# Modulation steps of the first layer: from the input projections into the attention, five to a head, and four raw tiles in the out projection

## The chip, the cores and the metric

The kernel runs on one core of one Trainium2 chip. The metric is the device time of one execution in microseconds (us); runs are compared by their median. The five engines each work through their own list of instructions in order: TensorE (PE in the profile, with its weight loads as PEld), VectorE (DVE), ScalarE (ACT), GpSimd (POOL) and SyncE (SP), which only issues transfers.

## What is computed

One inference step of a two-layer diffusion trunk, for 512 sample tokens and 128 prompt tokens with a model width of 1024. Cut to what matters here:

```python
def adaln(cvec, w_mod, b_mod):                       # six vectors of 1024 for each of two conditionings
    m = jax.nn.silu(cvec) @ w_mod + b_mod
    return m.reshape(cvec.shape[0], N_MOD, D_MODEL)[:, :, None, :]

for l in range(DEPTH):                               # two layers, the first with MLA attention
    mp, ms = adaln(c_ctx[None, :], w_mod[l], b_mod[l]), adaln(c, w_mod[l], b_mod[l])
    hs = modulate(rmsnorm(xs, norm_mix[l]), ms[:, 0], ms[:, 1])
    os_ = even_latent(hs, ...)                       # input projections, 12 heads, out projection w_out
    xs = xs + ms[:, 2] * os_
    hs = modulate(rmsnorm(xs, norm_ffn[l]), ms[:, 3], ms[:, 4])
    xs = xs + ms[:, 5] * conv_ffn(hs, ...)
```

The same is done for the prompt tokens with `mp`. The outputs are both token sets after a last norm and the new cache entries.

## The kernel before, in words

Activations are kept transposed, as eight tiles of 128 channels by W = 642 columns (512 sample columns, two of padding, 128 prompt columns), and are worked on in two halves, of 352 and 290 columns. All products are float32 split into a high and a low part: each term is three matmuls (`mm3`), and every weight tile that arrives raw is split by a cast on ScalarE (`whi` or `wo`) and a subtraction on VectorE or POOL (`wlo`, or the second `wo`; line 113).

The first layer goes through these stages: `start` (first norm, with modulation vectors 0 and 1), `mla_in` (the input projections, the norms of the low-rank queries `q` and of the latent `c`), `mla` (attention), `out_proj` (output projection, residual, the sum for the next norm), `ffn`. The second layer follows.

**Modulation steps.** Each vector `m` of a layer is a matrix-vector product for two conditionings, taken in steps. A step (`mod_step`) takes one raw tile of `w_mod`, 128 rows k by n columns, scales it by the conditioning and adds it to two accumulators: for the first conditioning one product on VectorE (line 316), for the second a scaling on ScalarE (313) and an addition on POOL (314). In mode "d" both are on VectorE; the first step of a sum (k = 0) runs on ScalarE alone (310), or in mode "d" on VectorE. Eight steps make the sum for n columns; the eighth is followed by two transposes (325) and two sums (326) on VectorE, the end of a sum. `mod_finish` turns a finished vector into columns with four small matmuls in two passes each (337) and adds the bias (275); inside `mods` it does so once a vector has been ready for five steps. `mods_in` gives a stage its number of steps, its ring of raw tiles and the queue that loads them: a load is issued when a step has freed its tile.

Before, `mla_in` runs the 16 steps of vector 2 (two sums of 512 columns) with a ring of three on ScalarE's queue, at the places marked `m` and `m.d` in the list `MLA_IN`; the attention runs the 32 steps of vector 4 (four sums of 256 columns) with a ring of three on SP; the out projection and the feed-forward run the rest (vectors 3 and 5, then layer 1) in steps of 512 columns with a ring of two on SP.

**Order.** In `mla_in` and `mla` the order of each engine's work is written out by hand. `MLA_IN` is a list of steps such as `p.q0.1` (projection q0, second half), `zc` (copy out), `sq` (squares), `sm` (sum of squares), `ln`, `nw` (root and Newton step), `sc` (scale and cast to the high part), `lo` (low part), `xc` (copy of a pooling projection out of its accumulator), `f` and `r` (fetch and split a weight), `m`. `MLA_UNITS` holds two such lists for the two halves of a head; unit t = 2 x head + half computes scores and exponentials of its own, and transposes and weighs those of the unit before. Heads with new keys (`k`) are those of odd number up to 9; new queries (`q`) are made up to head 9. Steps `m` run from t = 2 on, while there are any.

The out projection and the feed-forward are ordered by the scheduler of the framework, from the order of the program and its estimates; SP is ordered by it everywhere. `out_proj` makes eight outputs j for the first half and eight for the second; in its first pass each j loads its x tile and its weight tile (raw tiles: three in all). After each output come two modulation steps. `normed` holds the norm of the first half: the end of the modulation vectors, the sum of squares (359), then scale and shift (424, 437, 438) on VectorE and ScalarE, whose results `ha` and `hb` are the operands of the feed-forward.

Of the kernel before, what the change touches and what calls it, by code (L numbers as in the profile page):

```python
# [8 lines left out]
F32 = mybir.dt.float32  # L9
# [9 lines left out]
KT = 8  # L19
# [27 lines left out]

MLA_IN = """
m p.kr.0 m.d p.c0.0 p.kr.1 r.q0 f.q2 m.d rt p.c0.1 zc.c0 m.d m.d cx p.c1.0 p.c1.1 p.q0.0 sq.c0 zc.c1 r.q1 m.d sq.c1 sm.c r.q2 m.d m.d
f.xp0 ln.c f.wk f.xp1 nw.c.0 m nw.c.1 p.q0.1 p.q1.0 zc.q0 sq.q0 sc.c.1.0 p.q1.1 sc.c.1.1 lo.c.1.1 sc.c.0.1 r.wk p.q2.0 sc.c.0.0 rc  # L50
lo.c.0.0 zc.q1 lo.c.0.1 sq.q1 lo.c.1.0 m.d r.xp0 kp.1 kp.0 ke.1 p.q2.1 f.wq m.d r.xp1 f.wv ke.0 xz m zc.q2 p.xp0.0 m sq.q2 m sm.q p.xp0.1
ln.q r.wv nw.q.0 xc.0 xa.0 sc.q.0.0 p.xp1.0 r.wq p.xp1.1 iv.0 sc.q.0.1 xb.0 lo.q.0.0 sc.q.0.2 lo.q.0.1 nw.q.1 lo.q.0.2 m.d xm.0 sc.q.1.0
sc.q.1.1 xc.1 lo.q.1.0 sc.q.1.2 lo.q.1.1 xa.1 lo.q.1.2 xb.1 iv.1 m.d xm.1
"""


# [6 lines left out]
MLA_UNITS = ["""  # L63
v0.1 m sc.0 wl.0 sc.1 we.2 ou tu.0 tu.1 wl.1 ex.0 ex.1 lo.0 q lo.1 pm.1 no.0 no.1 tu.2 we.0 k m m pm.0 pa lo.2 ke v0.0 v qs ve we.1
""", """
sc.0 sc.1 pm.0 tu.0 lo.0 v0.1 tu.1 we.2 ou ex.0 wl.0 no.0 ex.1 v0.0 q tu.2 lo.1 no.1 wl.1 lo.2 we.0 m k ke we.1 v pa ve pm.1 qs
"""]
MLA_MODS = 32

ODD_NA = ["""  # L70
s.1 je s.0 m.0 j.3 jr.d t.0 pt l.0 j.5 m.1 je.d s.2 w.0 t.1 sp e.0 pl l.1 t.2 s.3 w.1 m.2 e.1 l.2 pw j.4 po sv r.1 br t.3 m.3 w.2 e.2
# [18 lines left out]
class Trunk:  # L90
# [359 lines left out]
    def out_proj(self, pool, l, oT, xsrc, after, early=()):  # L450

        nc = self.nc
        x, w, h, normed = [], [], self.acts(), None
        with self.pool(f"wout{l}") as wpool:
            for half in range(2):
                acc = None
                for j in range(KT):
                    if not half:
                        xt = self.T(pool, "x", [P, W], F32, 8)
                        nc.sync.dma_start(xt, xsrc[:, j, :])  # L460
                        x.append(xt)
                        split = early[j] if j < len(early) else self.fetch(self.i["w_out"][l, j], D, *(() if j < 3 else (wpool, ("wo", "wo"), 10)))
                        w.append(split(nc.gpsimd if j in OUT_LO[l] else nc.vector))
                    ps = self.PS("mm")
                    self.proj_half(ps, w[j], oT, half, order=(6, 7, 0, 1, 2, 3, 4, 5) if l == 0 else range(KT))
                    self.add_x(l, 2, j, x[j], ps[:, C0:C1], *HALF[half])
                    xj = x[j][:, slice(*HALF[half])]
                    acc = self.add_sqs(pool, half, j, xj, acc, nc.gpsimd if j in OUT_SQ[l][half] else nc.vector)
                    after()
                    if j == 1 and normed:  # L470
                        normed()

                def normed(half=half, acc=acc):
                    self.mod_finish("b")
                    self.norm_half(pool, h, x, acc, half, l, 3, 4)

            normed()
        return x, h
# [313 lines left out]
    def mla(self, pool, oT, wq):  # L792
# [97 lines left out]
        u1 = u2 = None  # L890
        for t in range(2 * MH + 2):
            hd, hf = divmod(t, 2)
            if t == 2:
                self.mod_finish("tr")
            u = None
            if hd < MH:
                u = Unit()
# [558 lines left out]
    def run(self):  # L1456
        tc, nc, i, o = self.tc, self.nc, self.i, self.o
        with ExitStack() as st:
# [35 lines left out]
            self.sink = const("sink", [P, 8], nc.sync)  # L1494
            self.nsink = cp.tile([P, 8], F32, name="nsink")
            nc.vector.tensor_scalar(out=self.nsink, in0=self.sink, scalar1=-1.0, scalar2=None, op0=ALU.mult)
            self.todo = deque(self.mods_of(0, (2,), 512) + self.mods_of(0, (4,), 256) + self.mods_of(0, (3, 5), 512))
            oT = self.acts()
            with self.pool("mla") as pool:
                self.mp, self.Q, self.V, self.wq, self.pm, self.pw = pool, {}, {}, {}, [], []  # L1500
# [4 lines left out]
                with self.psums(mla), self.pool("mla_att") as self.ap:  # L1505
                    self.qtab = self.T(self.ap, "qtab", [P, W])
                    nc.sync.dma_start(self.qtab, i["qtab"])
                    self.T(self.ap, "q32", [P, HA], F32, 2)
                    self.T(self.ap, "q", [P, W], F32R, 6)
                    wq = self.fetch(i["w_qk"][0], D)  # L1510
                    self.mods_in(self.ap, MLA_MODS, 3, nc.sync)
                    bias_full = self.bias_table(cp, dpool)
                    with tc.manual_schedule(engines=ENGINES):
                        self.mla(self.ap, oT, wq)
                        self.mod_finish("tr")
                        w_out = [self.fetch(i["w_out"][0, j], D) for j in range(3)]
            with self.psums(wide), self.pool("ffn0") as pool:
                self.todo.extend(self.mods_of(1, range(6), 512))
                self.mods_in(pool, len(self.todo), 2, nc.sync)
                x, h = self.out_proj(pool, 0, oT, i["xT"], lambda: self.mods_until("b", MODS_OUT, (0, 5)), w_out)  # L1520
                nh = self.acts()

                def tail(half, acc):
                    if half:
                        for k in range(KT):
                            nc.sync.dma_start(xd[:, k, :], x[k])
                    self.mod_finish("b")
                    self.norm_half(pool, nh, x, acc, half, 1, 0, 1)

                self.ffn(pool, 0, h, x, lambda n: self.mods("b", n), tail)  # L1530
# [796 lines left out]
```

## Time and profile before

| | |
|---|---|
| median of 3 runs | 1700.57 us (1700.29 to 1706.34) |
| the profiled execution | 1703.3 us, span 1701.5 us, clock 0.972 |
| TensorE busy | 1584.5 us (93%) |
| VectorE busy | 1260.4 us (74%) |
| ScalarE busy | 929.0 us (55%) |
| POOL busy | 770.5 us (45%) |
| transfers | 175.62 MB, 103 GB/s |

How to read it: the span is the time from the first to the last instruction of the program in the profiled execution. Times in the trace count from the span's start. In rows of groups stand line, engine, operation, output <- inputs, count, then busy time, mean in ns, and the idle time of the engine before them with what ended it. In rows in order of time stand start, duration and, in brackets, the idle time before and its releaser. Rows of waits name who waited for whom: us in total, times, the longest. Windows give the busy time of each engine with the number of its instructions, then TensorE's granted clock, the share of the DMA engines and GB/s.

### The profile page before, as it was taken

Reading aid. Unit: us, or ns where it says so; the run is one execution under the profiler, and the core shown is the slowest. Engines: PE = TensorE matmul, PEld = TensorE weight load, DVE = VectorE, ACT = ScalarE, POOL = GpSimd, SP = SyncE. Lnnn points to the kernel's source line nnn. Section 1 sums busy time; section 2 is a strip of 40 time slices with the busy share of each in tenths; the row PEclk is TensorE's granted clock in tenths of the full one; section 3 lists DMA queues with packets and bytes.
Section 4 is the critical chain, followed back from the end, with each engine's and each line's share of the span. In section 5 each row is a group of like instructions: output and inputs, shape, how many; then the busy total and the mean of one; then the engine's idle time right before and its main releaser. Section 6 shows DMA issues by size and latency. Waiting matters only on the chain.

```text
span 1701.5 us, 28135 instructions
## 1 busy us (share of the span) xinstructions
PE 1584.5 (93%) x10349; PEld 1512.7 (89%) x10349; DVE 1260.4 (74%) x2190; ACT 929.0 (55%) x1792; POOL 770.5 (45%) x704
## 2 busy tenths in 40 slices
PE   8878888889999999999997999998997999999996
PEld 2777777788899999999997999987997999999996
DVE  4896788768999778977638777776687666776766
ACT  3554777655555345544345678886565344444445
POOL 2154777554234332534063234663325456555543
PEclk9997999998999999999999999998999999999999
DMA  9431212044344444544225211114222122222221
GB/s 342 137 100 56 63 50 80 14 160 140 112 143 151 159 137 139 159 142 137 84 86 183 70 42 58 53 43 163 75 82 85 63 89 88 78 78 74 78 73 63
DMA packets 79032, 175.62 MB, mean 103 GB/s; under 512 B 11598, under 2 KB 29342, under 8 KB 78894
## 3 DMA queue, kind: packets, MB, share of 16 engines
q1 hardware_dynamic: 76398, 169.55, 30.9%
q10 hardware_dynamic: 2304, 4.20, 0.8%
q8 instruction: 82, 1.34, 0.3%
q14 instruction: 56, 0.46, 0.1%
q0 software_dynamic: 192, 0.07, 0.0%
HBM read 166.71 MB, written 8.03 MB: 103 GB/s over the span
## 4 chain that ended last, share of the span: by engine, by line
PE 49%; DVE 16%; issue 6%; ACT 5%; DMA 5%; POOL 1%; SPq 0%; DVEq 0%; ACTq 0%; POOLq 0%
PE p L1594 24%; PE mm L137 19%; DMA mraw<-in_w_mod_dram 4%; DVE wlo L113 2%; DVE acc L316 2%; PE sc L1209 1%; PE tr L1247 1%; PE o L1259 1%; DVE u L511 1%; DVE nt L424 1%; ACT whi L117 1%; DVE ha L438 1%; DVE g L113 1%; DVE v L1997 1%; ACT mt L313 1%
## 5 line engine op out<-in xcount | busy, mean ns | idle before, releaser
L314 POOL TENSOR_TENSOR acc<-acc,mt 128x512 f32<-128x512 f32 x115 | 175.5, 1526 | 266.1 <-ACT mt L313 251.3
L137 PE MATMUL mm<-ha,whi 128*128 128x352 f32 (+1 forms) x1168 | 287.5, 328 | 4.7 <-ACT ha L437 4.6
L137 PE MATMUL mm<-hb,whi 128*128 128x290 f32 (+1 forms) x1168 | 244.2, 302 | 1.1 <-ACT hb L437 1.1
L137 PEld LDWEIGHTS mm<-ha,whi 128*128 128x128 f32 (+1 forms) x1168 | 202.4, 190 | 6.5 <-ACT ha L437 4.7
L316 DVE SCALAR_TENSOR_TENSOR acc<-mraw,cs,acc 128x512 f32<-128x512 f32 (+1 forms) x165 | 169.7, 1035 | 47.5 <-DMA mraw<-in_w_mod_dram 45.9
L137 PEld LDWEIGHTS mm<-hb,whi 128*128 128x128 f32 (+1 forms) x1168 | 192.8, 191 | 4.0 <-issue 2.7
L137 PE MATMUL mm<-ha,wlo 128*128 128x352 f32 (+1 forms) x584 | 188.9, 324 | 0.0
L113 POOL TENSOR_TENSOR wlo<-raw,whi 128x1024 fp32r<-128x1024 f32 (+3 forms) x46 | 98.3, 2142 | 175.1 <-ACT whi L117 116.3
L137 PE MATMUL mm<-hb,wlo 128*128 128x290 f32 (+1 forms) x584 | 174.7, 299 | 0.0
L113 POOL TENSOR_TENSOR w<-raw,w 128x512 fp32r<-128x512 f32 (+1 forms) x68 | 90.3, 1339 | 172.9 <-ACT w L117 164.8
L137 PE MATMUL mm<-g,whi 128*128 128x352 f32 (+1 forms) x704 | 157.8, 311 | 7.0 <-DVE x L447 5.2
L117 ACT CAST whi<-raw 128x1024 fp32r<-128x1024 f32 (+3 forms) x117 | 116.0, 996 | 68.5 <-PE mm L137 52.0
L313 ACT ACTIVATE mt<-mraw,cs 128x512 f32<-128x512 f32 x115 | 81.7, 720 | 113.4 <-DMA mraw<-in_w_mod_dram 101.0
L1594 PE MATMUL p<-g,d 128*128 128x320 f32 (+1 forms) x912 | 140.0, 312 | 0.9 <-POOL d L113 0.9
L1594 PEld LDWEIGHTS p<-g,d 128*128 128x128 f32 x912 | 136.4, 189 | 2.3 <-POOL d L113 2.1
L1594 PE MATMUL p<-hb,w 128*128 128x322 f32 (+1 forms) x816 | 129.0, 313 | 7.4 <-DVE cg L1966 6.7
L1594 PEld LDWEIGHTS p<-hb,w 128*128 128x128 f32 x816 | 123.4, 191 | 8.3 <-DVE cg L1966 6.9
L137 PEld LDWEIGHTS mm<-g,whi 128*128 128x128 f32 x704 | 118.4, 189 | 9.5 <-ACT ha L437 3.9
L1594 PE MATMUL p<-ha,w 128*128 128x322 f32 x768 | 122.7, 314 | 1.5 <-ACT ca L1960 1.5
L1594 PEld LDWEIGHTS p<-ha,w 128*128 128x128 f32 x768 | 117.5, 192 | 1.9 <-ACT ca L1960 1.8
L137 PEld LDWEIGHTS mm<-hb,wlo 128*128 128x128 f32 (+1 forms) x584 | 112.5, 193 | 0.0
L137 PEld LDWEIGHTS mm<-ha,wlo 128*128 128x128 f32 (+1 forms) x584 | 110.1, 188 | 0.5
(332 smaller groups left out, 3763.1 us busy)
## 6 DMA issues: line engine op xcount, KB each, us to landing
raw<-in_w_up_dram SPq DMA_DIRECT2D x90, 512.0 KB, 3.6
mraw<-in_w_mod_dram SPq DMA_DIRECT2D x128, 256.0 KB, 2.9
raw<-in_w_out_dram SPq DMA_DIRECT2D x19, 512.0 KB, 4.0
raw<-in_w_in_odd_dram SPq DMA_DIRECT2D x18, 512.0 KB, 3.6
mraw<-in_w_mod_dram SPq DMA_DIRECT2D x16, 512.0 KB, 8.8
raw<-in_w_down_dram SPq DMA_DIRECT2D x16, 512.0 KB, 3.6
draw<-in_w_down_dram SPq DMA_DIRECT2D x40, 192.0 KB, 2.4
raw<-in_w_down_dram SPq DMA_DIRECT2D x16, 384.0 KB, 3.1
```

The source lines that it names most:

```text
L113: (engine or self.nc.vector).tensor_sub(lo, src, Fv(hi))
L117: self.nc.scalar.copy(hi, src)
L137: self.pe = self.nc.tensor.matmul(out, lhsT=l, rhs=r, start=k == 0, stop=k == n - 1)
L313: nc.scalar.activation(t, raw, AF.Copy, scale=s)
L314: nc.gpsimd.tensor_add(acc, acc, t)
L316: nc.vector.scalar_tensor_tensor(out=acc, in0=raw, scalar=s, in1=acc, op0=ALU.mult, op1=ALU.add)
L424: self.nc.vector.scalar_tensor_tensor(out=t[:, c], in0=x[k][:, c0:c1][:, c], scalar=self.mod[l][:, ma, k, v : v + 1], in1=rs[:, c], op0=AL ...
L438: nc.vector.scalar_tensor_tensor(out=lo[:, c], in0=t[:, c], scalar=ss, in1=Fv(hi[:, c]), op0=ALU.add, op1=ALU.subtract)
L511: nc.vector.scalar_tensor_tensor(out=u[:, 1:W], in0=ps[:, 0 : W - 1], scalar=cw[:, j, 0:1], in1=u[:, 1:W], op0=ALU.mult, op1=ALU.add)
L1209: nc.tensor.matmul(ps[:, c : c + n], lhsT=u.Q[:, a], rhs=x[e], start=e == 0, stop=e == 1)
L1247: nc.tensor.transpose(tp[:, j * P : (j + 1) * P], u.p[b][:, x : x + P], self.ident)
L1594: self.t.pe = self.nc.tensor.matmul(ps[:, 0:n], lhsT=l_, rhs=r[:, 0:n], start=first and m == 0, stop=last and m == count - 1, skip_group_c ...
```

## The change

`MLA_IN` loses the last eight of its 16 modulation steps, `xc.1` and `lo.q.0.2` move ahead of `nw.q.1`, and the second list of `MLA_UNITS` gets a second `m`, so that a head has five. Vector 2 is now one sum of 512 columns (in `mla_in`) and two of 256 (in the attention, eight steps each); the attention has 48 steps, from t = 2 to t = 20. Two calls of `mod_finish` go. In the out projection two x tiles are loaded ahead, each further weight tile is fetched right after a split, the norm of the first half stands behind output 2 of the second half instead of output 1, and the ring of raw modulation tiles, there and in the feed-forward, is four.

```diff
 m p.kr.0 m.d p.c0.0 p.kr.1 r.q0 f.q2 m.d rt ...
-f.xp0 ln.c f.wk f.xp1 nw.c.0 m nw.c.1 p.q0.1 p.q1.0 zc.q0 sq.q0 sc.c.1.0 p.q1.1 sc.c.1.1 lo.c.1.1 sc.c.0.1 r.wk p.q2.0 sc.c.0.0 rc
-lo.c.0.0 zc.q1 lo.c.0.1 sq.q1 lo.c.1.0 m.d r.xp0 kp.1 kp.0 ke.1 p.q2.1 f.wq m.d r.xp1 f.wv ke.0 xz m zc.q2 p.xp0.0 m sq.q2 m sm.q p.xp0.1
-ln.q r.wv nw.q.0 xc.0 xa.0 sc.q.0.0 p.xp1.0 r.wq p.xp1.1 iv.0 sc.q.0.1 xb.0 lo.q.0.0 sc.q.0.2 lo.q.0.1 nw.q.1 lo.q.0.2 m.d xm.0 sc.q.1.0
-sc.q.1.1 xc.1 lo.q.1.0 sc.q.1.2 lo.q.1.1 xa.1 lo.q.1.2 xb.1 iv.1 m.d xm.1
+f.xp0 ln.c f.wk f.xp1 nw.c.0 nw.c.1 p.q0.1 p.q1.0 zc.q0 sq.q0 sc.c.1.0 p.q1.1 sc.c.1.1 lo.c.1.1 sc.c.0.1 r.wk p.q2.0 sc.c.0.0 rc
+lo.c.0.0 zc.q1 lo.c.0.1 sq.q1 lo.c.1.0 r.xp0 kp.1 kp.0 ke.1 p.q2.1 f.wq r.xp1 f.wv ke.0 xz zc.q2 p.xp0.0 sq.q2 sm.q p.xp0.1
+ln.q r.wv nw.q.0 xc.0 xa.0 sc.q.0.0 p.xp1.0 r.wq p.xp1.1 iv.0 sc.q.0.1 xb.0 lo.q.0.0 sc.q.0.2 lo.q.0.1 xc.1 lo.q.0.2 nw.q.1 xm.0 sc.q.1.0
+sc.q.1.1 lo.q.1.0 sc.q.1.2 lo.q.1.1 xa.1 lo.q.1.2 xb.1 iv.1 xm.1
...
-sc.0 sc.1 pm.0 ... wl.1 lo.2 we.0 m k ke we.1 v pa ve pm.1 qs
+sc.0 sc.1 pm.0 ... wl.1 lo.2 we.0 m m k ke we.1 v pa ve pm.1 qs
-MLA_MODS = 32
+MLA_MODS = 48
...
-        x, w, h, normed = [], [], self.acts(), None
+        x, w, h, normed, raws = [], [], self.acts(), None, list(early)
+        def load_x():
+            if len(x) < KT:
+                x.append(self.T(pool, "x", [P, W], F32, 8))
+                nc.sync.dma_start(x[-1], xsrc[:, len(x) - 1, :])
+        for _ in range(2):
+            load_x()
...
-                        xt = self.T(pool, "x", [P, W], F32, 8)
-                        nc.sync.dma_start(xt, xsrc[:, j, :])
-                        x.append(xt)
-                        split = early[j] if j < len(early) else self.fetch(self.i["w_out"][l, j], D, ...)
-                        w.append(split(nc.gpsimd if j in OUT_LO[l] else nc.vector))
+                        load_x()
+                        w.append(raws[j](nc.gpsimd if j in OUT_LO[l] else nc.vector))
+                        if len(raws) < KT:
+                            raws.append(self.fetch(self.i["w_out"][l, len(raws)], D, wpool, ("wo", "wo"), 10))
...
-                    if j == 1 and normed:
+                    if j == 2 and normed:
...
-            if t == 2:
-                self.mod_finish("tr")
...
-            self.todo = deque(self.mods_of(0, (2,), 512) + self.mods_of(0, (4,), 256) + self.mods_of(0, (3, 5), 512))
+            self.todo = deque(self.mods_of(0, (2,), 512)[:KT] + self.mods_of(0, (2,), 256)[2 * KT :] + self.mods_of(0, (4,), 256) + self.mods_of(0, (3, 5), 512))
...
-                        self.mod_finish("tr")
...
-                self.mods_in(pool, len(self.todo), 2, nc.sync)
+                self.mods_in(pool, len(self.todo), 4, nc.sync)
```

More of the change, by code (lines that the diff above doesn't have):

```diff
@@ L65 @@
 """, """
-sc.0 sc.1 pm.0 tu.0 lo.0 v0.1 tu.1 we.2 ou ex.0 wl.0 no.0 ex.1 v0.0 q tu.2 lo.1 no.1 wl.1 lo.2 we.0 m k ke we.1 v pa ve pm.1 qs
+sc.0 sc.1 pm.0 tu.0 lo.0 v0.1 tu.1 we.2 ou ex.0 wl.0 no.0 ex.1 v0.0 q tu.2 lo.1 no.1 wl.1 lo.2 we.0 m m k ke we.1 v pa ve pm.1 qs
 """]
-MLA_MODS = 32
+MLA_MODS = 48
 ODD_NA = ["""
@@ L458, in out_proj @@
                     if not half:
-                        xt = self.T(pool, "x", [P, W], F32, 8)
-                        nc.sync.dma_start(xt, xsrc[:, j, :])
-                        x.append(xt)
-                        split = early[j] if j < len(early) else self.fetch(self.i["w_out"][l, j], D, *(() if j < 3 else (wpool, ("wo", "wo"), 10)))
-                        w.append(split(nc.gpsimd if j in OUT_LO[l] else nc.vector))
+                        load_x()
+                        w.append(raws[j](nc.gpsimd if j in OUT_LO[l] else nc.vector))
+                        if len(raws) < KT:
+                            raws.append(self.fetch(self.i["w_out"][l, len(raws)], D, wpool, ("wo", "wo"), 10))
                     ps = self.PS("mm")
```

## The prediction, made before the changed kernel was run

> **What bounds the kernel now.** I read the page first, then the busy time cut at the borders of the stages the change touches: 47 to 119 us the input projections, 119 to 141 their tail and the first attention queries, 141 to 357 the attention, 357 to 428 the out projection, then the first feed-forward.
>
> ```profile
> span 1701.5 us, 28135 instructions
> 47.00:119.00 72.00, 65.64 (x402) 61.47 (x402) 62.44 (x94) 41.25 (x84) 25.54 (x21) 0.94 0.41 123
> 119.00:141.00 22.00, 12.28 (x53) 11.35 (x51) 19.90 (x26) 5.07 (x11) 15.54 (x14) 0.61 0.51 154
> 141.00:357.00 216.00, 183.91 (x1227) 167.05 (x1227) 160.37 (x340) 145.20 (x344) 135.38 (x140) 0.96 0.14 46
> 357.00:428.00 71.00, 62.44 (x383) 60.76 (x382) 57.63 (x88) 37.36 (x59) 38.10 (x39) 0.90 0.50 168
> 428.00:830.00 402.00, 399.11 (x2687) 395.63 (x2686) 333.02 (x394) 198.30 (x270) 143.01 (x94) 1.00 0.44 141
> ```
>
> The columns are PE, PEld, DVE, ACT and POOL busy with their counts, then the granted clock. From 428 on TensorE is full (399.11 of 402), so what is won or lost before comes through to the end one for one. Ahead of it TensorE has holes: 9.7 of 22 us in the tail, at clock 0.61, and 8.6 of 71 in the out projection. Next, the waits of TensorE, for 47 to 141 us and then for 357 to 430:
>
> ```profile
> PE b L359 <- DVE sqz L404: 5.9, 4, 2.8
> PE tr L137 <- ACT px L683: 4.8, 1, 4.8
> PE tr L137 <- DVE q L774: 3.0, 1, 3.0
> PE tr L137 <- DVE qan L113: 1.9, 1, 1.9
> ```
> ```profile
> PE b L337 <- DVE mred L326: 4.2, 1, 4.2
> PE mm L137 <- DVE wo L113: 3.5, 1, 3.5
> ```
>
> Nearly all name VectorE: it is 19.90 of 22 us busy in the tail and sets its end.
>
> **Part 1, the projections: eight steps leave.** Of the 16 steps the first eight stay in place; the second eight (512 columns each) go, with their eight loads on ScalarE's queue. VectorE's products of 512 columns from 83 us on, which are those that go, then rows in order of time:
>
> ```profile
> L316 DVE SCALAR_TENSOR_TENSOR acc<-mraw,cs,acc 128x512 f32<-128x512 f32 x11 | 15.1, 1402 | 0.0
> ```
> ```profile
> 105.57 0.83 PE L359 MATMUL b<-sqz,ones 128*128 128x352 f32 x2 [2.78 <-DVE sqz L404]
> ...
> 107.58 0.52 DVE L378 TENSOR_TENSOR r<-r 128x352 f32<-128x352 f32 x1
> ...
> 122.47 3.50 DVE L316 SCALAR_TENSOR_TENSOR acc<-mraw,cs,acc 128x512 f32<-128x512 f32 x2
> ...
> 128.32 1.32 DVE L113 TENSOR_TENSOR qan<-z,qan 128x290 fp32r<-128x290 f32 x1 [0.15 <-ACT qan L629]
> 129.56 3.46 DVE L316 SCALAR_TENSOR_TENSOR acc<-mraw,cs,acc 128x512 f32<-128x512 f32 x2
> ...
> 135.61 0.52 DVE L774 TENSOR_TENSOR q<-tr,qtab 128x352 f32<-128x352 f32 x1
> ...
> 141.82 0.31 PE L137 MATMUL sc<-kh,q 128*128 128x320 f32 x1
> ```
> ```profile
> 136.19:141.82 5.63, 5.63 (x28) 5.63 (x28) 3.53 (x7) 2.21 (x6) 2.23 (x3) 0.57 0.82 246
> ```
>
> The 11 VectorE products that go took 15.1 us, besides two transposes and two sums. Their gain is read from the chain. The wait of 2.78 us for the query squares falls away, because the products that delayed the squares are gone and TensorE reaches the sum at 102.8 (105.57 less 2.78): everything behind starts 2.8 earlier, the first Newton step at 104.8 instead of 107.58. From there to the last low part of the queries (128.32 + 1.32 = 129.6) VectorE runs without a longer pause; without the 3.50 us at 122.47 the end is 129.6 - 2.8 - 3.5 = 123.3. The first query product, at 135.61, then follows at once, since the last step (3.46 us, then transposes and sums to 135.61) is gone too: 12.3 us earlier. Not all of it reaches the first score: with the queries of the second half TensorE still has two of its four query products (18 matmuls) and 18 value matmuls ahead of the score. 27 of them took 5.63 us at clock 0.57 (the window's 28th is the score), 0.21 each, so 36 take 7.5, and the score comes at 123.3 + 7.5 = 130.8 instead of 141.8: **-11.0 us**. The edits of order serve this: `xc.1` put ahead of the second Newton pass frees the accumulator behind the 4.8 us wait, and the third low part ahead of that pass lets the first two query products run early; counted in the 7.5. Late next are the second half's low parts at 123.3, for which TensorE will wait. The eight loads and ScalarE's share of the steps lay beside VectorE (ScalarE 41.25 of 72 busy), at nothing. Ends: -8 (only the 3.50 and 3.46 us of late steps, and 1 us of the wait) to -12.3.
>
> **Part 2, the attention: 16 steps of 256 columns come, four to five a head.** The same bytes, now 16 loads of 128 KB on SP. A step is one product on VectorE, one scaling on ScalarE, one addition on POOL; two of the 16 begin a sum and run on ScalarE alone. VectorE by form, 160 to 325 us, then the busy times of three heads:
>
> ```profile
> L316 DVE SCALAR_TENSOR_TENSOR acc<-mraw,cs,acc 128x256 f32<-128x256 f32 x28 | 25.7, 918 | 0.3
> L113 DVE TENSOR_TENSOR kl<-tr,kh 64x512 fp32r<-64x512 f32 x10 | 6.9, 688 | 9.6 <-ACT kh L117 9.6
> L113 DVE TENSOR_TENSOR kl<-tr,kh 64x256 fp32r<-64x256 f32 x9 | 3.8, 419 | 4.2 <-ACT kh L117 4.2
> L325 DVE STREAM_TRANSPOSE mraw<-acc 128x256 f32<-128x256 f32 x8 | 3.6, 446 | 8.3 <-POOL acc L314 8.1
> L326 DVE TENSOR_REDUCE mred<-mraw 128x8 f32<-128x256 f32 x8 | 3.4, 420 | 0.3
> ```
> ```profile
> 220.01:237.09 17.08, 13.73 (x96) 12.44 (x95) 13.65 (x29) 11.97 (x29) 14.05 (x16) 1.00 0.27 88
> 307.89:325.86 17.97, 14.00 (x87) 12.59 (x88) 13.20 (x30) 9.54 (x22) 6.99 (x9) 0.91 0.01 3
> 325.86:337.38 11.52, 9.70 (x71) 8.72 (x70) 8.72 (x20) 7.92 (x20) 5.25 (x5) 1.00 0.13 43
> ```
>
> The full bill on VectorE is 14 x 0.918 = 12.9 us, and two more ends of a sum, each two transposes, two sums and a wait for POOL's last addition (8.1 over four): 2 x (0.89 + 0.84 + 2.03) = 7.5; together 20.4. What covers it? In a head without new keys (220.01) VectorE is 13.65 of 17.08 busy, and a wait for POOL is most of the rest: there a step costs its whole 0.92. In a head with keys it waits 13.8 us over five heads for the keys' high parts, right behind the place of the added step: there a step is mostly free. Head 9 (307.89, no steps so far) has 4.8 us idle, head 10 (325.86) 2.8. Four steps in heads without keys 3.7; four with keys 0.5; five in head 9 half covered, 2.3; three in head 10 with a sum's end 2.8 + 3.8 - 2.8 = 3.8; the other added end 3.8; less the two that are VectorE's for nothing, 1.8; less about 2 where two of the moved ends fall into heads with keys: **+10.5 us**. Ends: +4 (only heads 10 and the like pay) and the bill, +20.4. POOL's 14 additions and ScalarE's 18 scalings lie beside this; SP has a ring of three here as before, and the attention's own weights are fetched two units ahead. The two `mod_finish` calls cost nothing: the one at t = 2 moves its eight matmuls to a later unit by the rule of five steps' age, the last finds nothing.
>
> One row shows why 0.918 and not 0.47: two steps in a row take 1.86, a single one 0.47; the second of the pair, 1.39, falls beside POOL's multiplications of the softmax.
>
> ```profile
> 205.89 1.86 DVE L316 SCALAR_TENSOR_TENSOR acc<-mraw,cs,acc 128x256 f32<-128x256 f32 x2
> ...
> 215.52 0.47 DVE L316 SCALAR_TENSOR_TENSOR acc<-mraw,cs,acc 128x256 f32<-128x256 f32 x1
> ```
> ```profile
> 206.05 2.81 POOL L830 TENSOR_TENSOR p<-p,s 128x640 f32<-128x640 f32 x2 [3.37 <-DVE s L823]
> ```
>
> The Trainium skill (GPSIMD Engine Reference, Key points) says that POOL shares its SBUF interfaces with VectorE and contends with VectorE instructions that have two SBUF inputs, as this product has. By that the pair's second step is slowed by POOL, and the trace agrees with its 1.39. It speaks against this edit: work of that kind moves to where POOL adds and multiplies throughout.
>
> **Part 3, the out projection.** Two x tiles are loaded ahead, each weight tile three outputs ahead of its use, the ring of raw modulation tiles is four, and the first half's norm stands behind the third output of the second half. Below are windows, rows in order of time, the 120 matmuls of five outputs of the second half, and POOL's additions from 357 to 402 us.
>
> ```profile
> 353.60:377.20 23.60, 23.60 (x149) 23.27 (x147) 14.55 (x16) 11.71 (x19) 15.37 (x13) 1.00 0.65 215
> 410.00:428.00 18.00, 17.14 (x123) 16.55 (x122) 18.00 (x38) 8.10 (x17) 4.40 (x18) 1.00 0.12 40
> ```
> ```profile
> 370.35 0.43 SPq L739 DMA_DIRECT2D raw<-in_w_out_dram  x1
> 379.48 1.21 DVE L113 TENSOR_TENSOR wo<-raw,wo 128x1024 fp32r<-128x1024 f32 x1
> 401.76 1.46 PE L337 MATMUL b<-mred,sel 128*128 128x16 f32 x6 [4.18 <-DVE mred L326]
> 444.62 0.98 PE L137 MATMUL mm<-hb,whi 128*128 128x290 f32 x2 [0.26 <-ACT hb L437]
> ```
> ```profile
> L137 PE MATMUL mm<-hb,wo x120: 289/297/302, 409.1 to 425.1; 128*128 128x290 f32 x120
> ```
> ```profile
> L314 POOL TENSOR_TENSOR acc<-acc,mt 128x512 f32<-128x512 f32 x14 | 21.7, 1550 | 11.3 <-ACT mt L313 11.0
> ```
>
> The seventh weight tile is issued only at 370.35, behind x and modulation loads, and its low part ends at 380.7: the 3.5 us wait. The second wait, before 401.76, is for the end of modulation product 3, paced by loads. An output of the first half takes 24 x 23.60/149 = 3.8 us, of the second 16.0/5 = 3.2. Without stalls the second half begins at 353.6 + 8 x 3.8 = 384.0 and its third output ends at 393.6: there the sum of product 3 stands, 8.1 before 401.76. Is it ready? POOL, with 21.7 us of additions less the 11.0 of waiting for loads, is done 11.0 before 401.8, at about 391. But from 401.76 to the last gate at 444.62 VectorE is the bound (18.00 of 18), so TensorE's freed time counts only as far as this chain starts earlier: 8.1, and one output's update less behind the sum, 0.4: **-8.5 us**. TensorE alone would gain 425.1 - (384.0 + 8 x 3.2) = 15.5, less some 2 for the norm's own matmuls: 13. Ends: -2 (only part of the weight wait) and -13. Four kilobytes more of SBUF and the deeper ring in the feed-forward cost nothing: TensorE is full there.
>
> **Sum.** -11.0 + 10.5 - 8.5 = -9.0. The profiled execution took 1703.3 us (span 1701.5), 2.7 over the median of 1700.57; taken off the median: 1691.5 us, just over half a per cent, which is about what a measurement of this kernel can tell from no change.
>
> **Rivals.** (a) The attention hides the steps: +4 instead of +10.5, 1685. For it: head 9's idle time. Against: the heads without keys. (b) The out projection does not follow, -2: modulation product 3 remains late, or the scheduler's new order delays the norm: 1698, no change. For it: only the two waits are TensorE's, the chain behind is VectorE's. (c) On the other side: in the attention every added product falls beside POOL. 14 x 1.39 + 7.5 = 27 with no cover: -11.0 + 27 - 8.5 = +7.5, 1708. From 19.5 us on the change loses, from 28 by more than half a per cent. For it the pair's row; against it the single steps at 0.47 and the keys' waits. The Trainium skill's rule (GPSIMD Engine Reference, Key points), if it held for every step, would be this case. (d) The change does not do what it says in the projections, another wait taking VectorE's place (-8 there): 1694.5.
>
> **Chances.** The forecast 0.34 and (a) 0.18 make 0.52 faster by over half a per cent; (b) 0.22, (d) 0.07 and the bill of 20.4 in full (1691.5 + 9.9 = 1701.4) 0.12 make 0.41 within; (c) and what lies beyond it 0.07 slower. Range: from (a) with part of the out projection's 13, 1682, to the full bill with some of (b), 1703.
>
> **What would show it.** The first score near 131 us; VectorE's products of 256 columns 42 instead of 28, near 0.9 us each, six sum ends, the attention from first score to first out projection matmul some 222 us long instead of 211.8; the weight wait gone and the sum of product 3 within 41 us of the first output. Wrong if the attention grows by over 19 us or the gate at 444.62 moves less than the start of the out projection.

## The result, and the profile after

| | before | after |
|---|---|---|
| median of five runs each | 1703.14 us (1700.29 to 1706.34) | 1733.42 us (1730.62 to 1734.62) |
| ratio after / before | | 1.0184, 95% interval 1.0170 to 1.0199 |
| the profiled execution | 1703.3 us, span 1701.5 | 1730.62 us, span 1728.8 |

The change makes the kernel 30 us slower; the forecast was 1691.5 us (counted from 1700.57, the median of the first three runs of before), and its range ended at 1703. First the page of the kernel after, then its windows, cut at the first score (134.02), the first matmul of the out projection (376.75) and the first feed-forward matmul on `hb` (470.75), called the gate from here on. The prediction's gate, the last matmul that waits for `hb` (444.62 before), is a few us later. Columns: PE, PEld, DVE, ACT, POOL busy, then granted clock, DMA share, GB/s.

```profile
span 1728.8 us, 28214 instructions
```
```profile
112.00:134.02 22.02, 13.60 (x73) 12.14 (x73) 19.58 (x22) 6.28 (x14) 17.65 (x17) 0.77 0.59 176
134.02:376.75 242.73, 189.34 (x1201) 173.02 (x1199) 180.69 (x360) 151.42 (x357) 145.48 (x149) 0.90 0.14 44
376.75:470.75 94.00, 78.29 (x474) 76.02 (x474) 88.82 (x115) 48.11 (x79) 55.31 (x53) 0.93 0.53 176
```

The same two stages of the kernel before:

```profile
141.82:353.63 211.81, 179.72 (x1200) 162.86 (x1199) 159.38 (x338) 143.08 (x339) 133.18 (x135) 0.96 0.13 43
353.63:439.43 85.80, 77.24 (x474) 75.45 (x474) 67.97 (x108) 43.94 (x73) 44.59 (x46) 0.92 0.48 161
```

So the 27.3 us between the two spans are: the first score 7.8 earlier, the attention 30.9 longer, the out projection up to the gate of the feed-forward 8.2 longer instead of shorter, and the rest 4.0 shorter (1258.1 instead of 1262.1). In the attention VectorE has 21.3 us more work, and TensorE's idle time (span less busy) grew by as much: nothing was covered. TensorE's busy time grew by another 9.6 us, for the same matmuls at a granted clock of 0.90 instead of 0.96 (and so again in `x2_old_out` below: 189.5 us, 0.90). Waits of the kernel after in the attention, of TensorE, of VectorE and of ScalarE (us in total, times, longest):

```profile
PE tr L846 <- DVE pt L850: 19.1, 13, 4.8
PE sc L137 <- ACT kh L117: 12.2, 5, 5.5
```
```profile
DVE mraw L325 <- POOL acc L314: 14.3, 6, 4.5
```
```profile
ACT acc L310 <- DVE mraw L325: 8.2, 6, 4.4
```

Two of these as they were before:

```profile
PE sc L137 <- ACT kh L117: 1.5, 3, 0.7
```
```profile
DVE mraw L325 <- POOL acc L314: 8.1, 4, 2.2
```

TensorE's wait for the keys is hardly there before, and VectorE's for POOL never lasted over 2.2 us. One place shows how it comes about: the end of a sum in unit 11, rows in order of time for each engine (start, duration, in brackets the idle time ahead and its releaser).

```profile
251.41 2.34 POOL L113 TENSOR_TENSOR wlo<-raw,whi 128x1024 fp32r<-128x1024 f32 x1
253.71 0.72 POOL L314 TENSOR_TENSOR acc<-acc,mraw 128x256 f32<-128x256 f32 x1
...
254.46 0.45 DVE L325 STREAM_TRANSPOSE mraw<-acc 128x256 f32<-128x256 f32 x1 [4.49 <-POOL acc L314]
...
254.94 0.51 ACT L310 ACTIVATE acc<-mraw,cs 128x256 f32<-128x256 f32 x1 [4.37 <-DVE mraw L325]
...
256.35 0.35 ACT L117 CAST kh<-tr 64x256 fp32r<-64x256 f32 x1
...
256.75 0.64 PE L137 MATMUL sc<-kh,q 128*128 128x320 f32 x1 [5.47 <-ACT kh L117]
```

The eighth step's addition stands on POOL behind a weight split of 2.34 us. VectorE, at the transposes, waits 4.49 us for it. ScalarE's first step of the next sum waits for the accumulators, with the keys' cast `kh` behind it, and TensorE waits 5.47 us for its scores. With four steps to a head a sum of eight ended with the last step of every second head. With five, counted from the lists, the six sums end in units 4, 8, 11, 14, 17 and 20, only one of them (17) with the last step of a head, and in units 8, 11 and 14 the next sum's first step follows in the same unit.

### The profile page after: what moved, and what is told of

The parts are those of the page before. It is cut to its first block, busy times and chain, and to the rows that moved or that the text cites. A ratio compares the mean times of both kernels' runs of the same rounds, so it can differ in the third digit from the quotient of the medians.

```text
span 1728.8 us, 28214 instructions
## 1 busy us (share of the span) xinstructions
PE 1587.5 (92%) x10349; PEld 1517.7 (88%) x10349; DVE 1285.9 (74%) x2197; ACT 935.0 (54%) x1805; POOL 786.0 (45%) x715
## 4 chain that ended last, share of the span: by engine, by line
PE 56%; DVE 12%; issue 5%; ACT 5%; POOL 1%; DMA 1%; SPq 0%; DVEq 0%; ACTq 0%; POOLq 0%
PE mm L137 28%; PE p L1598 22%; DVE acc L316 2%; PE sc L1214 1%; PE tr L1252 1%; PE o L1264 1%; DVE nt L424 1%; DVE ha L438 1%; DVE v L2001 1%; DVE x L447 1%; DMA mraw<-in_w_mod_dram 1%; DVE sq L404 1%; DVE w L113 0%; DVE pt L113 0%; ACT whi L117 0%
## 5 line engine op out<-in xcount | busy, mean ns | idle before, releaser
L314 POOL TENSOR_TENSOR acc<-acc,mt 128x512 f32<-128x512 f32 x112 | 180.5, 1612 | 266.8 <-ACT mt L313 242.7
L316 DVE SCALAR_TENSOR_TENSOR acc<-mraw,cs,acc 128x512 f32<-128x512 f32 (+1 forms) x168 | 187.1, 1118 | 12.1 <-DMA mraw<-in_w_mod_dram 8.2
L113 DVE TENSOR_TENSOR wlo<-raw,whi 128x1024 fp32r<-128x1024 f32 x71 | 96.5, 1359 | 22.9 <-ACT whi L117 22.1
## 6 DMA issues: line engine op xcount, KB each, us to landing
mraw<-in_w_mod_dram SPq DMA_DIRECT2D x48, 128.0 KB, 2.2
```

Source lines behind the costliest of these rows:

```text
L113: (engine or self.nc.vector).tensor_sub(lo, src, Fv(hi))
L314: nc.gpsimd.tensor_add(acc, acc, t)
L316: nc.vector.scalar_tensor_tensor(out=acc, in0=raw, scalar=s, in1=acc, op0=ALU.mult, op1=ALU.add)
```

## The experiments

### Which stage costs

`x1_out_only` is before with the out projection's edits alone (with the ring of four); `x2_old_out` is the changed kernel with the old `out_proj` and a ring of two.

> The kernel before with only the out projection's edits (two x tiles ahead, each weight tile fetched after a split, the norm behind output 2, a ring of four). Theory: the deeper ring lets more modulation steps run inside the out projection, and VectorE, full there, comes to its own work later: from the first out projection matmul to the last gate about 98 us instead of 91, the whole +5 to +9 us. Rival A (the prediction's): the stage follows the earlier fetches, -8.5 us. Rival B: the out projection was slow in the changed kernel only because it was reached in another state (a late weight tile, a lower granted clock): within 2 us of before.

> The changed kernel with the old out projection (ring of two, old order of loads, norm behind output 1): projections and attention of the change alone. Theory: -8 from the projections and +31 from the attention, so +21 to +25 us against before. Rival B of the run with the out projection alone (the stage is slow because of what comes ahead of it): about +31 us, since the out projection would stay slow.

Measured: 1708.13 us, 1.0028 (1.0012 to 1.0044), and 1726.31 us, 1.0140 (1.0125 to 1.0156). The parts add up. In the first the gate comes 94.2 us after the first out projection matmul (98.2 up to the last matmul that waits for `hb`, which is what the expectation's 98 and 91 count to), in the second 86.4: the out projection is slow for its own edits, whatever comes ahead of it. The prediction's -8.5 is refuted.

### The place of the ends: no instruction more, 15 us

`x3_five_only` is before with the second `m`; `MLA_MODS` stays 32.

```diff
-... wl.1 lo.2 we.0 m k ke we.1 v pa ve pm.1 qs
+... wl.1 lo.2 we.0 m m k ke we.1 v pa ve pm.1 qs
```

> The kernel before with five modulation steps to a head instead of four, the number of steps unchanged (32, which now end in head 7 instead of head 9). Not one instruction more on any engine; only the places differ, and the ends of the sums fall in the middle of a unit instead of behind the last step of a head. Theory (misplaced ends cost: VectorE waits for POOL's last addition, ScalarE's first step of the next sum waits for the accumulators, and the keys' cast behind it is late): +8 us or more, the attention 220 us or longer instead of 211.8. Rival (only the number of steps and POOL's contention count): within 2 us of before.

Measured: 1717.22 us, 1.0090 (1.0065 to 1.0114). Its attention and two of its waits:

```profile
142.62:369.82 227.20, 182.28 (x1201) 166.32 (x1199) 165.26 (x337) 142.15 (x338) 133.61 (x135) 0.94 0.13 40
```
```profile
DVE mraw L325 <- POOL acc L314: 11.0, 4, 4.5
```
```profile
PE sc L137 <- ACT kh L117: 7.8, 4, 5.5
```

15.4 us longer than before, with the same steps. Half of the attention's 30.9 us is the place of the steps alone.

### Sixteen steps more, ends in place: 2.5 us in the attention

`x4_four_a_head` is the changed kernel with the second `m` taken out again: 48 steps, over units 2 to 25.

> The changed kernel with four steps to a head instead of five: the same 48 steps, spread over units 2 to 25, each sum of eight again ending with the last step of every second head. Theory (misplaced ends): the attention grows by the steps' own VectorE time where it is not idle, 222 to 230 us instead of some 243, and the whole is 13 to 21 us below the changed kernel. Rival (the number of steps and contention): the attention stays at 238 us or more, the whole within 5 us of the changed kernel.

Measured: 1706.29 us, 1.0022 (1.0013 to 1.0032), 27 below the change. Its attention:

```profile
133.18:347.45 214.27, 176.56 (x1192) 159.60 (x1191) 171.44 (x353) 151.25 (x356) 144.60 (x148) 0.97 0.17 52
```

214.3 instead of 211.8 us, 7.7 less than the lower bound that was expected. Units 3 to 17, whose steps are those of before, mostly have the same length to a few hundredths of a us. From the first score of unit 18 on the attention takes 7.0 us more, and 3.9 come back in units 1 and 2: unit 1 no longer holds the eight matmuls of `mod_finish` (TensorE busy 7.6 us with 50 matmuls, 9.0 with 58 before), and unit 2 runs at a granted clock of 1.00 instead of 0.81. The 2.5 us are not the whole price: only 41 of the 42 products and ten of the twelve transposes fall into this window; the end of the last sum and the finish of vector 4 come behind the first out projection matmul, and `x9_four_old_out` below shows that stage later by 4.7. In the attention the number of steps costs little.

### Which wait: two pairs of accumulators, then held ends

Both on the 1717 us kernel. The first gives the accumulators a second pair; the second also holds the two transposes and two sums back until the last step of the head, and the transposes write to tiles of their own (`mt`) instead of the raw tile.

```diff
-            self.acc = [self.T(pool, f"acc{v}", [P, n]) for v in range(2)]
+            self.acc = [self.T(pool, f"acc{v}", [P, n], F32, 2 if mode == "i" else 1) for v in range(2)]
...
+        if mode == "i":
+            self.held.append((l, m, c, n, self.acc))
...
+                    if hf and um == 2:
+                        self.mod_flush()
```

> Before with five steps to a head, as in the run that cost 15 us, and two pairs of accumulators instead of one: the first step of the next sum, on ScalarE, no longer waits until VectorE has transposed the sum before. Theory (the end in mid-unit costs by two waits, VectorE's for POOL and ScalarE's for the accumulators, the second holding up the keys' cast and with it the scores): ScalarE's waits of 4.4 us and the scores' of 5.5 us go, VectorE's up to 4.5 us stay; some 4 to 9 of the 15 us come back. Rival A (VectorE's wait for POOL alone is the cause): 2 us or less come back. Rival B (a fifth step in a head is too much wherever its end is): 2 us or less here, and in the next run too.

> The same, and the end of a sum (two transposes, two sums) is held back until the last step of the head, where the kernel before has it; the transposes write to tiles of their own. The five steps to a head stay. Theory (the place of the ends costs): the waits of VectorE for POOL fall to some 8 us in sum and at most 2.2 each, and 9 us or more of the 15 come back. Rival B (five steps to a head cost, not the ends): within 4 us of the run with five steps to a head.

Measured: 1716.38 us, 1.0078 (1.0056 to 1.0101), and 1704.78 us, 1.0015 (1.0004 to 1.0025). Waits of the first, then the window and a wait of the second, where line numbers are a few higher:

```profile
PE sc L137 <- DVE kl L113: 5.6, 2, 4.6
```
```profile
DVE mraw L325 <- POOL acc L314: 11.0, 4, 4.5
```
```profile
141.30:355.00 213.70, 180.55 (x1201) 163.85 (x1200) 163.08 (x338) 142.19 (x339) 133.41 (x135) 0.95 0.13 42
```
```profile
DVE mt L333 <- POOL acc L315: 3.6, 1, 3.6
```

The theory of two waits falls: with a second pair ScalarE no longer waits, but the keys' low part `kl` stands on VectorE behind the same transposes, and TensorE waits for that instead. What is left as the cause is VectorE's wait for POOL ahead of the transposes, in that place: the kernel before has 8.1 us of it too, in four waits of at most 2.2. With the ends held it is down to 3.6 us, and 12.4 of the 15 us come back, with five steps to a head still. What the transposes' own tiles did in this was not tried apart.

`x11_after_held` does the same to the whole change.

> The changed kernel whole, five steps to a head, but with the ends of the sums held until the last step of a head and with two pairs of accumulators. Theory: the attention falls from some 243 us to 215 to 224 us, the whole by 18 us or more against the changed kernel, to about +8 us or less against before. Rival (16 more steps cost by their number): 10 us or less come back.

Measured: 1707.62 us, 1.0036 (1.0021 to 1.0051), 26 us below the change; the attention takes 218.3 us. VectorE's products are 42 there too. The theory holds on the change itself.

### The out projection piece by piece

On before: the ring of four alone; loads and norm place with a ring of two; the norm's place alone (`j == 2` instead of `j == 1`).

> Before with a ring of four raw modulation tiles in the out projection and the feed-forward, nothing else. Theory: the ring lets modulation steps run ahead into the out projection, where VectorE is full: +4 to +8 us, as much as all edits of the out projection together. Rival (the order of loads or the norm's place cost, the ring doesn't): within 2 us of before.

> Before with the out projection's earlier loads and the norm behind output 2, but a ring of two. Theory (the ring is what costs): 0 to -5 us, since the wait of 3.5 us for the seventh weight tile is met by an earlier load. Rival (loads or norm cost): +4 us or more.

> Before with the first half's norm behind output 2 of the second half instead of output 1, nothing else. Theory (the norm's place costs one output, since the scale and shift on VectorE that gate the feed-forward begin that much later): +2 to +5 us. Rival (the loads cost what the run with loads and norm lost): within 1 us of before.

Measured: 1713.24 us, 1.0061 (1.0043 to 1.0079); 1706.27 us, 1.0018 (1.0004 to 1.0032); 1705.30 us, 1.0013 (0.9997 to 1.0029). The gates come at 98.0, 90.6 and 88.1 us, against 85.8. The ring costs most, 11 us alone, more than all edits together; the earlier loads mend part of that. The norm's place moves the gate by 2.3 us, though its time can't be told from no change; the loads, with the ring of two, won nothing, against the theory. Two rows of the kernel with the ring alone, and two groups of VectorE from the first output to the gate, of before and then of the change:

```profile
384.77 0.43 SPq L739 DMA_DIRECT2D raw<-in_w_out_dram  x1
...
391.59 0.95 PE L137 MATMUL mm<-ha,wo 128*128 128x352 f32 x2 [11.13 <-ACT wo L117]
```
```profile
L316 DVE SCALAR_TENSOR_TENSOR acc<-mraw,cs,acc 128x512 f32<-128x512 f32 x21 | 21.9, 1042 | 8.3 <-DMA mraw<-in_w_mod_dram 8.2
L404 DVE TENSOR_TENSOR sq<-sq,sq 128x352 f32<-128x352 f32 (+1 forms) x12 | 8.5, 706 | 1.6 <-ACT sq L402 1.5
```
```profile
L316 DVE SCALAR_TENSOR_TENSOR acc<-mraw,cs,acc 128x512 f32<-128x512 f32 x28 | 36.7, 1310 | 0.3
L404 DVE TENSOR_TENSOR sq<-sq,sq 128x352 f32<-128x352 f32 (+1 forms) x12 | 12.4, 1036 | 0.6 <-ACT sq L402 0.6
```

Two costs. With the ring alone the seventh weight tile is issued 31.6 us after the first output (first matmul at 353.2) instead of 16.7, since 16 modulation loads are ahead of it on SP in this stage instead of 6, and TensorE waits 11.1 us. And VectorE has more to do: in the change 28 products instead of 21. Vector 3 needs only 14: the others are the feed-forward's, which the scheduler brings forward as soon as their tiles are there. While POOL is busier (55.3 us instead of 44.6) they take 1310 ns instead of 1042, and the squares' additions 1036 instead of 706.

To tell the two apart, `x13_ring4_late` (on before) keeps the ring of four but gives the feed-forward's steps tiles of their own, where the out projection's weights lie until it is done; `x14_four_late2` and `x15_four_late4` do that, with rings of two and four, on a version with four steps to a head (below).

```diff
-                self.mods_in(pool, len(self.todo), 2, nc.sync)
+                self.mods_in(pool, 2 * KT, 4, nc.sync)
...
+                with self.pool("mods0") as mpool:
+                    self.mods_in(mpool, len(self.todo), 4, nc.sync)
+                    self.ffn(pool, 0, h, x, lambda n: self.mods("b", n), tail)
```

> Before with a ring of four in the out projection, as in the run that cost 10 us, but only the 16 steps of vector 3 are loaded there; the feed-forward's steps load into tiles of their own, which the out projection's weights occupy until it is done. Theory (the ring costs because feed-forward steps run inside the out projection, on a full VectorE): VectorE has about 15 products there instead of 28, the gate comes 80 to 88 us after the first out projection matmul, and the whole is within 3 us of before or below it. Rival (the ring costs because more modulation loads stand ahead of the seventh weight tile on SP): the 11 us wait for that tile stays, +6 us or more.

> Four steps to a head, the change's projections and order of loads, ring two, norm behind output 1, and the feed-forward's modulation steps kept out of the out projection as in the run beside this. Theory: with 5 or more products fewer on VectorE in the out projection the gate comes 3 to 8 us earlier, and the whole is 3 us or more below before. Rival (the 16 steps of vector 3, paced by their loads, set the stage): within 2 us of before.

> The same with a ring of four in the out projection, where now only vector 3's steps can fill it. Theory: the wait of 5.4 us for the end of vector 3's sum shrinks, since its loads run ahead, and the whole is 1 to 5 us below the run with a ring of two. Rival (the loads of the ring stand ahead of the weight tiles): 2 us or more above it.

Measured: 1718.51 us, 1.0084 (1.0071 to 1.0097); 1711.65 us, 1.0042 (1.0028 to 1.0055); 1704.38 us, 1.0002 (0.9991 to 1.0013). Of the first, from the first output to the gate at 444.7:

```profile
353.30:444.70 91.40, 75.06 (x475) 73.05 (x474) 69.28 (x100) 42.06 (x69) 39.44 (x39) 0.91 0.38 126
```
```profile
PE mm L137 <- DVE mt L325: 12.5, 1, 12.5
```

Both theory and rival are half right, and the theory's times were missed. The late weight tile stays, as the rival had it: the row names a transpose that ended late on VectorE, but the weight load beside it waited 12.8 us for the tile's cast on ScalarE, which ended at 391.7. With most of the feed-forward's steps out (18 products are left) VectorE has 69.3 us to do instead of 87.0, and the gate comes at 91.4 instead of 98.0. But what is won is paid later: from the gate to the end it takes 1272.4 us instead of 1261.3. Most of that lies right behind the gate: in the first 115.3 us TensorE is busy 106.6, against 113.8 before, and VectorE 109.6 against 105.8. The same in the other two: the gate at 88.7 and at 83.2 (before: 85.8), and then 1271.6 and 1271.0. The first of them missed theory and rival alike. So with these steps the feed-forward and what follows take some 9 to 10 us longer than before. Between these two the ring of four gains 7 us, more than expected, where only vector 3's steps can fill it.

### A version that gains

`x9_four_old_out` and `x10_four_loads` have the change's projections and 48 steps, four to a head; the first with the old out projection, the second with the change's loads, a ring of two and the norm behind output 1.

> The change's projections and its 48 attention steps, four to a head instead of five, with the old out projection. Theory: the stages add up: first score 8 us earlier, attention 2 to 3 us longer, out projection as before, so -4 to -7 us against before. Rival (what is won ahead is lost in the out projection, where vector 4 is now finished): within 2 us of before.

> The same with the change's order of loads in the out projection (two x tiles ahead, each weight tile fetched after a split), the ring still two and the norm still behind output 1. Theory (the norm's place and the ring are what cost, the loads gain): 1 to 4 us below the run with the old out projection. Rival (the loads cost): 2 us or more above it.

Measured: 1703.10 us, 1.0002 (0.9991 to 1.0013), and 1702.30 us, 1.0003 (0.9991 to 1.0015): as before, as the rival of the first had it, and no difference between the two. The first score comes 8 us earlier, the attention takes 2.3 to 3.4 us more, and the out projection takes 2.4 to 4.7 us more up to the gate (it now also holds the end of vector 4). The expected sum missed that last term.

Then the projections, on the second of these: `xc.1` and `lo.q.0.2` back in their old places, and then one more line, for the copy ahead of the second pooling's last addition.

```diff
-            nc.scalar.copy(s2[0:64, 0 : n - d // 2], s[0:64, d // 2 : n])
+            (nc.scalar.copy if k == "0" else nc.gpsimd.tensor_copy)(s2[0:64, 0 : n - d // 2], s[0:64, d // 2 : n])
```

> Projections: the run with four steps to a head and the change's loads, with the two moved entries of the projections' list put back (the copy of the second pooling projection behind the second Newton pass and the first scalings of the second half; the third low part behind that pass). Theory (POOL's pooling additions, started early by the moved copy, stretch VectorE's norm of the second half and eat 3 us of the gain): the second Newton pass takes 2.5 us or less instead of 4.9, and the first score comes at 131 to 134 us. Rival (as the prediction had it, the moved copy frees the accumulator and helps): the first score comes at 135 us or later.

> The run with the old order in the projections (four steps to a head, the change's loads), and the one copy of the second pooling that ScalarE made after a wait for POOL is made by POOL itself. Theory (VectorE's low parts are done at about 124 there, and the first score waits only because ScalarE stands at that copy for 5.7 us with the queries' cast behind it): ScalarE's wait is gone and the first score comes at 129.5 to 131.5 us instead of 134.6, the whole 2 to 5 us below the run with four steps and the change's loads. Rival (the queries wait for something else as late): the first score at 134 us or later.

Measured: 1704.43 us (one run); 1697.03 us, 0.9972 (0.9962 to 0.9982). First the rows of the change, then of these two:

```profile
117.95 2.36 POOL L113 TENSOR_TENSOR wlo<-raw,whi 128x1024 fp32r<-128x1024 f32 x1
118.20 2.28 DVE L380 TENSOR_SCALAR r<-r 128x290 f32<-128x290 f32 x1
120.27 1.35 POOL L696 TENSOR_TENSOR ps<-px 128x663 f32<-128x663 f32 x1
120.51 1.43 DVE L381 TENSOR_TENSOR r<-r,r 128x290 f32<-128x290 f32 x1
...
126.95 1.04 DVE L113 TENSOR_TENSOR qan<-z,qan 128x290 fp32r<-128x290 f32 x2
...
134.02 0.31 PE L137 MATMUL sc<-kh,q 128*128 128x320 f32 x1
```
```profile
117.85 0.46 DVE L381 TENSOR_TENSOR r<-r,r 128x290 f32<-128x290 f32 x1
...
122.04 1.74 DVE L113 TENSOR_TENSOR qan<-z,qan 128x290 fp32r<-128x290 f32 x1 [1.10 <-ACT qan L636]
...
127.69 0.74 ACT L704 COPY ps<-ps 64x653 f32<-64x653 f32 x1 [5.68 <-POOL ps L699]
128.33 0.48 ACT L117 CAST q<-q 128x352 fp32r<-128x352 f32 x1
...
134.56 0.47 PE L137 MATMUL sc<-kh,q 128*128 128x320 f32 x1
```
```profile
121.52 1.75 DVE L113 TENSOR_TENSOR qan<-z,qan 128x290 fp32r<-128x290 f32 x1 [1.09 <-ACT qan L636]
...
129.88 0.31 PE L137 MATMUL sc<-kh,q 128*128 128x320 f32 x1
```

In the change VectorE's second Newton pass, four instructions, takes 4.9 us (116.96 to 121.94), beside POOL's split and pooling additions. In the old order it takes 3.0, a little over the 2.5 expected, and the last low part is done at 123.8 instead of 128.0, as the theory had it. Still the first score comes no earlier, and so outside both expectations: ScalarE stands 5.7 us at a copy that waits for POOL's additions, with the queries' cast behind it. With the copy on POOL the score comes at 129.9, and the whole is 0.28% faster than before, the only kernel here that beats it.

### All runs, by stage

First score, length of the attention, first out projection matmul to the first feed-forward matmul on `hb`, and from there to the end, in us, each from its profiled execution.

| kernel | median | first score | attention | to the gate | rest |
|---|---|---|---|---|---|
| before | 1703.14 | 141.8 | 211.8 | 85.8 | 1262.1 |
| after | 1733.42 | 134.0 | 242.7 | 94.0 | 1258.1 |
| `x1_out_only` | 1708.13 | 142.5 | 210.4 | 94.2 | 1258.7 |
| `x2_old_out` | 1726.31 | 134.0 | 243.0 | 86.4 | 1261.4 |
| `x3_five_only` | 1717.22 | 142.6 | 227.2 | 86.7 | 1259.5 |
| `x4_four_a_head` | 1706.29 | 133.2 | 214.3 | 93.1 | 1262.3 |
| `x6_five_held` | 1704.78 | 141.3 | 213.6 | 86.6 | 1262.3 |
| `x7_ring_only` | 1713.24 | 142.6 | 210.6 | 98.0 | 1261.3 |
| `x11_after_held` | 1707.62 | 133.5 | 218.3 | 94.2 | 1258.3 |
| `x10_four_loads` | 1702.30 | 133.3 | 214.1 | 88.2 | 1264.1 |
| `x17_pool_copy` | 1697.03 | 129.9 | 213.9 | 89.0 | 1261.9 |

## Why the prediction was wrong

**Part 1, -11.0 predicted, -7.8 measured: right mechanism, one term mis-sized.** The wait for the squares went, and the first Newton step came at 104.90, where 104.8 was forecast. The step that failed is "from there to the last low part VectorE runs without a longer pause, so 123.3": it ended at 128.0, because with the two moved entries POOL runs beside the second norm and stretches it (`x16_old_order`: 123.8 without them). What was left behind it took 6.0 us, not 7.5. In `x17_pool_copy` the rest of the sum comes out: last low part at 121.52 + 1.75 = 123.3, score at 129.9. The edits of order, which the prediction counted as a help, were what took the missing 3 to 4 us, together with a copy on ScalarE that it had not looked at. The -7.8 is the -8 of rival (d) in number only: VectorE was still the last, only slower.

**Part 2, +10.5 predicted, +30.9 measured: the step "what covers it" failed, twice.** VectorE's bill was read somewhat low: 42 products at 996 ns where 0.9 us was forecast, 21.3 us more busy time against 16.3 (the 20.4 less its 4.1 of waiting). The terms of the cover, as they stand, add up to 10.3, not 10.5.

```profile
L316 DVE SCALAR_TENSOR_TENSOR acc<-mraw,cs,acc 128x256 f32<-128x256 f32 x42 | 41.8, 996 | 1.7 <-ACT acc L310 0.8 <-DMA mraw<-in_w_mod_dram 0.4
```

But the prediction priced every end of a sum at the 2.03 us of waiting that the ends of before had, and even took 2 us off "where two of the moved ends fall into heads with keys". Those four ends stood at the last step of a head, the best of the places tried. The price of an end belonged to its place, not to the end: moving them together with their steps cost 15.4 us without one instruction more (`x3_five_only`), 12 of which came back when the ends were held back to their old place in the head (`x6_five_held`). A head with keys was not cover for an end: there the keys were the next ones to be late. On the other hand 16 more steps with their ends in place cost 2.5 us in the attention (`x4_four_a_head`), below the +4 of rival (a), though part of their bill moved into the out projection. Rival (c), every product beside POOL, came near in number, 27 against 30.9, but it is not what happened: the products grew from 918 to 996 ns on the average, not to 1390, and TensorE's new waits stand at the ends of the sums.

**Part 3, -8.5 predicted, +8.2 at the gate measured: wrong sign.** By the prediction's own gate, the last matmul that waits for `hb`, it is +7.1 (98.1 us instead of 91.0). Three steps failed. "Each weight tile three outputs ahead of its use" is the program's order, not SP's: in the change the seventh tile is issued 18.6 us after the first output, later than before (16.7), behind ten modulation loads instead of six.

```profile
395.30 0.43 SPq L746 DMA_DIRECT2D raw<-in_w_out_dram  x1
```
```profile
PE b L359 <- DVE sq L404: 5.8, 1, 5.8
PE mm L137 <- DVE wo L113: 4.6, 1, 4.6
```

TensorE's wait for a weight tile's low part, which was to go, grew from 3.5 to 4.6 us, and a wait for VectorE's squares came up, 5.8 us instead of 0.9.

The sum of product 3, forecast within 41 us of the first output, came after 52. And "the deeper ring costs nothing" looked at SBUF and at the feed-forward alone: its tiles let 14 feed-forward products into the out projection where 7 were, in the stage where the prediction itself had named VectorE as the bound at the end. VectorE was 88.8 of 94.0 us busy, instead of 68.0 of 85.8. The norm behind output 2 cost some 2 us at the gate (`x12_norm_place`) where the prediction's chain had it for nothing. Rival (b) named the scheduler's new order, but priced the part at -2.

Of the signs that the prediction set up, the first three it named were met or nearly so (a score at 134 for 131, 42 products near 0.9, six ends); the attention, 242.7 us long where some 222 were named, the weight wait, which stayed, and the sum of product 3 spoke against it. What stays open: whether the feed-forward's loss when its steps are kept out of the out projection is VectorE's or the loads' was not tried.

## What to carry to other kernels

Work that runs in rounds of its own length (here eight steps and an end) inside a hand-ordered pattern (here heads of two units) has a phase: a change of its rate moves every wait to another place, so price the ends at the places where they will fall, and let the rounds end where the pattern has room. A deeper ring is not only memory: it can let a scheduler bring later work into the stage that is full now, and put its loads ahead of that stage's own. Before counting the gain of a wait that goes, follow each of the other engines through that place, for ScalarE or POOL can hold the end as late.

## What the runs showed of the hardware that was not expected

Here a VectorE instruction with a single input from SBUF was held to the end of a POOL instruction. In the change the scaling of the second Newton pass (290 columns) took 2.28 us, 118.20 to 120.48, and ended 0.17 after POOL's split (117.95 to 120.31). The same line of the first pass, where POOL does nothing, took 0.34 for more columns:

```profile
106.02 0.34 DVE L380 TENSOR_SCALAR r<-r 128x352 f32<-128x352 f32 x1
```

In the old order it took 0.48, to 117.81, beside a short POOL instruction, again ending 0.17 after it:

```profile
117.33 0.48 DVE L380 TENSOR_SCALAR r<-r 128x290 f32<-128x290 f32 x1
```
```profile
117.19 0.45 POOL L714 TENSOR_TENSOR o<-o,px 128x128 f32<-128x128 f32 x1
```

The Trainium skill (SBUF — State Buffer, "SBUF: two separate sides") says that the port pair which VectorE and POOL share is a lock, held for a whole instruction by whoever starts first, while the other blocks, and that VectorE takes it in its two-port modes as well as with two inputs in SBUF. The trace agrees in both places, and in a third: before the same scaling took 0.78 us, 120.44 to 121.22, and ended 0.16 after a POOL instruction (119.68 to 121.06). Each time the delay is about the rest of POOL's instruction and not a share of it. That this instruction ran in a two-port mode no row shows. The prediction had looked at instructions with two inputs alone.
